# Eight experts of a mixture in one sequence: heavy blocks cut in halves between light ones

## The chip, the cores and the metric

The kernel runs on one core of a Trainium2 chip. The metric is the device time of one execution in microseconds (us). The engines are named as the profile names them: PE (TensorE, matmuls; PEld is its weight load), DVE (VectorE), ACT (ScalarE), POOL (GpSimd), SP (SyncE, which here only issues DMAs). "Part" means 1 MB of expert weights in this text, the unit in which they are loaded.

## What is computed

Two layers of a trunk with D = 1024 channels on T = 256 tokens. Each layer is a token mixer and a channel mixer; layer 0 has a dense channel mixer, layer 1 a mixture of 8 experts of which each token uses 2. All the change lies in that mixture. In the reference (cut):

```python
def _swiglu(t, w1, w3, w2):
    return (jax.nn.silu(t @ w1) * (t @ w3)) @ w2
...
    logits = (t @ w_router + b_router).astype(jnp.float32)
    top_val, top_idx = lax.top_k(logits, TOP_K)
    top_w = jax.nn.softmax(top_val, axis=-1)
    gates = jnp.sum(jax.nn.one_hot(top_idx, N_EXPERTS, dtype=jnp.float32) * top_w[..., None], axis=1)
    for e in range(N_EXPERTS):
        out = out + gates[:, e:e + 1].astype(t.dtype) * _swiglu(t, w1[e], w3[e], w2[e])
```

w1 and w3 of an expert are 1024 x 2816, w2 is 2816 x 1024, all in float32: 33 parts an expert, 264 in all. The kernel computes an expert only for the tokens that chose it.

## The kernel before

Up to the router the program is a fixed sequence. `route` (L1021) ranks the tokens of every expert and gives each expert a class `ov` by its count (up to 64, up to 128, up to 208, more). The loop at L1417 then goes over the experts in their own order. For each it loads the class into a register of all five engines and branches (L1426 to L1435) into one of four programs:

- `small` (L1168), up to 64 tokens. The tokens are gathered by a matmul with a one-hot matrix (`xg`, L1175) and turned (L1183). The 2816 hidden columns go in 11 blocks j. A block's first product `s` (L1200) takes two parts (w1 and w3 of 256 columns each), its second product `y` (L1218) one part of w2. The weights are the moving operand, straight from the loaded float32 part, and the 64 tokens are held in two column tiles of 64, which work on different columns. In order: transposes of the last block's gated values (`gT`, L1212; ACT copies them from PSUM, L1215), the first product of block j, the second product of block j - 1.
- `middle` (L1245), up to 128 tokens: the same with whole-array matmuls of 512 columns (`s` L1267, `gT` L1279, `y` L1286), and the weights split in a rounded high and a low half: ACT writes the high half `wh` (L210), DVE the low half `wl` (L211), in pieces of 128 x 1024.
- `many` (L1316), up to 208 or 256 tokens: tokens as the moving operand in the first product (`s` L1350 and L1352), weights moving in the second (`y` L1372), weights split as above, and gated values split by `split` (L248).
- After its last block an expert's rows are scaled (`ys`) and returned to the tokens by matmuls (`sc`, L1240, L1311, L1412), and `add_back` (L1140) adds them to `x_t`.

All weights come through SP's DMA queue into a ring of 15 slots of one part. `load_raw` (L186) takes the next slot in the order of use; `refill` (L178) is called after each stage and issues DMAs (L183) in that same order for the slots that are free. The first 15 parts are all of expert 0 and are issued before the router is done. `finish` (L1145) writes the output after the last expert.

## Time and profile before

| | us |
|---|---|
| median of 3 runs (1570.55 to 1571.85) | 1571.26 |
| the profiled execution | 1569.24 |
| its span in the trace | 1567.5 |
| PE busy in the span | 1371.7 (88%) |
| DVE busy | 881.6 (56%) |
| ACT busy | 605.2 (39%) |
| share of 16 DMA engines on SP's queue | 67.9% |

The span is the time between the first and the last record in the trace; the profiled execution's own time is 1.74 us longer. All rows read below are from this one execution. The experts occupy the span from 744 us to its end. PE's busy time comes from modelled ends of matmuls, so a busy PE is not necessarily at its full rate. The page counts bytes by queue (403.34 MB on SP's) and gives DMA's GB/s by slices, which is what the weight stream is read from.

### The profile page before, as it was taken

The numbers are of one execution on the slowest core, as the hardware profiler recorded it, in microseconds if no ns is written. First come the engines' busy times: TensorE is split into PE (matmuls) and PEld (weight loads), VectorE is DVE, ScalarE is ACT, GpSimd is POOL, SyncE is SP. The second block draws the span as 40 slices with busy tenths as digits, with TensorE's granted clock in tenths as the row PEclk, the third lists the DMA queues.
The fourth block names the chain that finished last, engine by engine and source line by source line (L and its number), as shares of the span: only waits on it lengthen the run. The fifth ranks groups of instructions, "written<-read, shape, count | busy, mean of one in ns | idle before, by whom it ended". The sixth has DMA issues, their size and how long they took to land.

```text
span 1567.5 us, 24755 instructions
## 1 busy us (share of the span) xinstructions
PE 1371.7 (88%) x9903; PEld 1139.8 (73%) x9903; DVE 881.6 (56%) x1443; ACT 605.2 (39%) x1115; POOL 318.9 (20%) x295
## 2 busy tenths in 40 slices
PE   4788999799998878988998949999799897979796
PEld 3676998699997777988665648988677574747474
DVE  7888679897777778687111036666588301010102
ACT  3453564354455534644111125555477211111112
POOL 0568019986201625050000000000000000000000
PEclk8898999799999899999998969999899998989899
DMA  7454356477776344479899975666399599999993
GB/s 285 174 190 160 125 188 212 136 258 240 261 257 223 133 136 135 166 244 403 359 419 416 419 290 189 215 203 203 130 348 351 212 420 416 419 416 419 417 419 122
DMA packets 60379, 420.37 MB, mean 268 GB/s; under 512 B 6688, under 2 KB 6688, under 8 KB 11296
## 3 DMA queue, kind: packets, MB, share of 16 engines
q1 hardware_dynamic: 56160, 403.34, 67.9%
q0 software_dynamic: 4032, 14.68, 2.8%
q8 instruction: 100, 1.64, 0.4%
q14 instruction: 87, 0.71, 0.1%
HBM read 416.94 MB, written 1.05 MB: 267 GB/s over the span
## 4 chain that ended last, share of the span: by engine, by line
PE 70%; DVE 18%; issue 6%; DMA 2%; ACT 2%; DVEq 0%; SPq 0%; ACTq 0%
PE s L1200 16%; PE mm L231 15%; PE y L1218 8%; DVE wl L211 6%; PE s L1350 4%; PE y L1372 4%; PE facc L971 3%; PE s L1267 3%; PE s L1352 2%; PE y L1286 2%; DMA raw<-in_w13m_dram 2%; DVE acc L309 1%; PE mm L716 1%; PE xg L1175 1%; DVE x_t L1141 1%
## 5 line engine op out<-in xcount | busy, mean ns | idle before, releaser
L211 DVE TENSOR_TENSOR wl<-raw,wh 128x1024 fp32r<-128x1024 f32 (+1 forms) x290 | 391.0, 1363 | 118.6 <-ACT wh L210 116.2
L210 ACT ACTIVATE wh<-raw 128x1024 fp32r<-128x1024 f32 (+1 forms) x290 | 302.3, 1057 | 252.1 <-PE mm L231 102.1
L231 PE MATMUL mm<-hh,wh 128*128 128x256 f32 x864 | 250.7, 292 | 5.1 <-ACT hh L250 2.9
L231 PE MATMUL mm<-hh,wl 128*128 128x256 f32 x864 | 249.7, 290 | 5.8 <-DVE wl L211 5.8
L1200 PE MATMUL s<-raw,xs 128*64 128x256 f32 x1920 | 250.1, 390 | 3.4 <-DVE xs L1187 3.4
L231 PE MATMUL mm<-hl,wh 128*128 128x256 f32 x864 | 249.5, 289 | 2.0 <-DVE hl L251 1.0
L1200 PEld LDWEIGHTS s<-raw,xs 128*64 128x64 f32 x1920 | 183.8, 140 | 48.2 <-issue 13.9
L1205 DVE TENSOR_TENSOR sg<-sg,s 64x256 f32<-64x256 f32 x66 | 28.0, 424 | 318.6 <-ACT sg L1204 269.8
L231 PEld LDWEIGHTS mm<-hh,wl 128*128 128x128 f32 x864 | 169.4, 196 | 9.8 <-DVE wl L211 6.3
L231 PEld LDWEIGHTS mm<-hh,wh 128*128 128x128 f32 x864 | 169.0, 196 | 9.4 <-ACT hh L250 3.3
L231 PEld LDWEIGHTS mm<-hl,wh 128*128 128x128 f32 x864 | 169.2, 196 | 3.7 <-DVE hl L409 1.5
L1218 PE MATMUL y<-raw,gT 128*64 128x512 f32 x520 | 143.1, 600 | 4.7 <-ACT gT L1215 4.7
L1204 ACT ACTIVATE sg<-s 64x256 f32<-64x256 f32 x66 | 24.8, 375 | 314.2 <-PE s L1200 314.2
L1350 PE MATMUL s<-xe,wh 128*128 128x416 f32 x352 | 107.2, 368 | 2.0 <-DVE sg L1360 1.7
L1352 PE MATMUL s<-xe,wl 128*128 128x208 f32 x352 | 91.0, 258 | 0.0
L309 DVE SCALAR_TENSOR_TENSOR acc<-raw,cond,acc 128x512 f32<-128x512 f32 x91 | 81.4, 894 | 1.6
L1218 PEld LDWEIGHTS y<-raw,gT 128*64 128x64 f32 x520 | 51.1, 136 | 40.9 <-issue 30.5
L317 POOL TENSOR_TENSOR araw<-araw,cond 128x1024 f32<-128x1024 f32 x28 | 62.3, 2229 | 71.8 <-DMA araw<-in_w_ada_dram 71.8
L1350 PEld LDWEIGHTS s<-xe,wh 128*128 128x128 f32 x352 | 66.2, 188 | 4.3 <-DVE sg L1360 2.4
L1352 PEld LDWEIGHTS s<-xe,wl 128*128 128x128 f32 x352 | 67.3, 191 | 0.4
L971 PE MATMUL facc<-fgh,wh 128*128 128x256 f32 x352 | 62.9, 281 | 0.2 <-ACT wh L210 0.2
L321 POOL TENSOR_TENSOR araw<-araw,araw 128x1024 f32<-128x1024 f32 x21 | 58.2, 2773 | 1.6
(513 smaller groups left out, 2369.0 us busy)
## 6 DMA issues: line engine op xcount, KB each, us to landing
raw<-in_w13m_dram SPq DMA_DIRECT2D x160, 1024.0 KB, 13.8
raw<-in_w2m_dram SPq DMA_DIRECT2D x87, 1024.0 KB, 13.7
raw<-in_w_ada_dram SPq DMA_DIRECT2D x32, 1024.0 KB, 5.1
raw<-in_w_in_dram SPq DMA_DIRECT2D x28, 1024.0 KB, 5.0
raw<-in_w13d_dram SPq DMA_DIRECT2D x22, 1024.0 KB, 5.0
late<-in_w13m_dram SPq DMA_DIRECT2D x16, 1024.0 KB, 16.2
araw<-in_w_ada_dram POOLq DMA_DIRECT2D x28, 512.0 KB, 4.6
raw<-in_w2d_dram SPq DMA_DIRECT2D x11, 1024.0 KB, 5.0
```

What stands on the lines that cost most here:

```text
L210: S.activation(hv, rv, AF.Copy)
L211: V.tensor_tensor(lv, rv, hv.bitcast(F32), op=ALU.subtract)
L231: PE.matmul(ps, lhsT=a[k][:, c0:c0 + P], rhs=b[:, k, :], start=k == 0 and i == 0 and o % 2 == 0, stop=k == n - 1 and i == 2 and o % 2 == 1)
L309: V.scalar_tensor_tensor(acc0, raw[:, k, :], c, acc0, op0=ALU.mult, op1=ALU.add)
L317: G.tensor_tensor(raw, raw, cond[:, r0:r0 + 2].unsqueeze(2).broadcast_to([P, 2, 512]), op=ALU.mult)
L321: G.tensor_tensor(acc, acc, raw, op=ALU.add)
L971: PE.matmul(o, lhsT=a[k][:, oc * P:(oc + 1) * P], rhs=b[:, k, :], start=j == 0 and oc % 2 == 0 and k == 0 and i == 0, stop=j == NB - 1 and ...
L1200: PE.matmul(ps[h][hf[h], 0:256], lhsT=xe4[:, k // 4, k % 4, :], rhs=w[k][:, 256 * h:256 * h + 256], start=k == 0, stop=k == KC - 1, tile_p ...
L1218: PE.matmul(y[h][hf[h], :], lhsT=g[:, k, :], rhs=w[k][:, 512 * h:512 * h + 512], start=j == 0 and k == 0, stop=j == NB - 1 and k == 1, til ...
L1350: PE.matmul(ps[:, 0:2 * nb], lhsT=hs[k][:, c], rhs=x.rearrange("p i s -> p (i s)"), start=k == 0, stop=False)
L1352: PE.matmul(ps[:, nb:2 * nb], lhsT=ls[k][:, c], rhs=x[:, 0, :], start=False, stop=k == KC - 1)
L1372: PE.matmul(y[b][n][0:s1 - s0, :], lhsT=g[:, k, s0:s1], rhs=w[w_][k][:, n * 512:n * 512 + 512], start=j == 0 and k == 0 and i == 0, stop=j ...
```

## The change

After the ranks, `ordered` (L1075 of the new kernel) sorts experts 1 to 7 by count and puts them in seven places behind expert 0 by `PLACE`. `si` holds which expert stands in each place; SP reads it into registers, and a part's DMA takes its expert from the register. `fi` says whether the counts fit the first list of `SIZES`, the second, or neither. A single branch (L1832) chooses: `straight` with the first list, with the second, or `general`, the old loop with its branches (now with a class of up to 32 besides).

`straight` is one sequence over all experts. Light experts (32 or 64 slots) follow each other in the order `LIGHT`, one block to a step, and the last block of one shares a step with the first of the next. A light expert of 32 uses four column tiles of 32, with 128 columns in a matmul of the first product and 256 in the second. Into these steps the 22 halves of each heavy expert are put (H1 its first product, H2 its second), a half every 1.1 steps: the 208-slot expert over steps 5 to 28, then three steps with none, the 128-slot expert over steps 32 to 55. All light blocks of steps 5 to 31 are of 32 slots; from step 33 on they are of 64. Gathers and returns are generators of which a piece runs after each step (`tick`). The ring has 14 slots, and only the 14 parts of expert 0 that fit are loaded before the sort. The sequence of parts in the ring follows the sequence of steps.

```diff
+SIZES = ((32, MANY, 32, 128, 64, 64, 64, 32), (64, MANY, 64, 128, 64, 64, 64, 64))
+HEAVY = (1, 3)
+LIGHT = (0, 2, 7, 5, 6, 4)
+LEAD, PACE, GAP = 5, 1.1, 3
...
+            w, e, (j, i), rows = parts[filled[0]]
+            if e and not experts:
+                return
+            src = w[0, j] if e == 0 else w[bass.ds(experts[e - 1], 1), j].squeeze(0)
+            if i is not None:
+                src = src[:, 4 * i:4 * i + 4, :]
             b = ring[filled[0] % len(ring)].rearrange("p (r c) -> p r c", r=rows)
             nc.sync.dma_start(b, src)
             filled[0] += 1
...
+        V.tensor_tensor(above[:, 0:7, 0:7], key[:, 1:8].unsqueeze(1).broadcast_to([P, 7, 7]),
+                        key[:, 1:8].unsqueeze(2).broadcast_to([P, 7, 7]), op=ALU.is_gt)
+        V.memset(rank[:, 0:1], -1.0)
+        V.reduce_sum(rank[:, 1:8], above[:, 0:7, 0:7], axis=AX.X)
...
+        def bring(o, row):
+            V.tensor_tensor(above, ow, row.unsqueeze(1).broadcast_to([P, 8, 8]), op=ALU.mult)
+            V.reduce_sum(o, above, axis=AX.X)
...
+        V.tensor_tensor(over, seq[:, 1:2, :].broadcast_to([P, 2, 8]), cov('limits').rearrange("p (a e) -> p a e", a=2),
+                        op=ALU.is_gt)
+        V.reduce_max(fl, over, axis=AX.X)
+        V.tensor_tensor(fi, fl[:, 0:1], fl[:, 1:2], op=ALU.add)
...
-        MR = 11
...
+        MR = 10
...
-        for e in range(NE):
-            rv = nc.values_load(ov[0:1, e:e + 1], engines=ENGS, min_val=0, max_val=3,
-                                skip_runtime_bounds_check_because="it is a sum of three comparisons")
...
-            with tc.If(rv < 1) as c:
-                arm(small)
-            with c.Else():
-                with tc.If(rv < 2) as c2:
-                    arm(middle)
-                with c2.Else():
-                    with tc.If(rv < 3) as c3:
-                        arm(lambda e: many(e, MANY))
-                    with c3.Else():
-                        arm(lambda e: many(e, T))
...
+        NARROW, WIDE = ("mm0", "mm0", "mm1"), ("mm0", "mm0", "mm1", "ms1", "ms1")
+        def wk(name):
+            return bank(work[0], name)
...
+            def turn_g():
+                ps = wk("gT")
+                for k in range(2 * n // 64):
+                    PE.transpose(ps[:, k * 64:(k + 1) * 64], st["sg"][hi, k * P:(k + 1) * P], ident[hi, hi],
+                                 tile_position=(64, 0))
+                st["g"] = mo.tile([P, 2, n], F32, name=nm("gS"), tag="gS", bufs=2)
+                S.activation(st["g"], ps[:, 0:2 * n].rearrange("p (k s) -> p k s", k=2), AF.Copy)
...
+            def stage1(j):
+                w = rows_of(w13m[0, j], KC, 512)
+                ps = wk("s1")
+                for k in range(KC):
+                    for g in range(G_):
+                        PE.matmul(ps[gr[g], 0:c_], lhsT=st["xe"][:, k // cb, k % cb, :], rhs=w[k][:, c_ * g:c_ * g + c_],
+                                  start=k == 0, stop=k == KC - 1, tile_position=(0, n * g))
                 refill()
...
+            def stage2(j):
+                if j == 0:
+                    st["y"] = bank(("mm1",), "y")
+                w = rows_of(w2m[0, j], 2, 1024)
+                for k in range(2):
+                    for h in range(G_):
+                        PE.matmul(st["y"][gr[h], 0:w_], lhsT=st["g"][:, k, :], rhs=w[k][:, w_ * h:w_ * h + w_],
+                                  start=j == 0 and k == 0, stop=j == NB - 1 and k == 1, tile_position=(0, n * h))
+                refill()
...
+            def stage1(j):
+                hs, ls = load_w(w13m[0, j], 8, 512, 2)
+                if n > P:
+                    gh, gl = (mo.tile([P, 2, n], F32R, name=nm("ghl"), tag="gT", bufs=2) for _ in range(2))
+                    for c in range(2):
+                        t = mo.tile([P, 2, n], F32, name=nm("sg"), tag="pt", bufs=2)
+                        for i in range(2):
+                            ps = wk("s1")
+                            o = slice((2 * i + c) * P, (2 * i + c + 1) * P)
+                            for k in range(KC):
+                                x = st["xe"][k // 4][:, k % 4]
+                                PE.matmul(ps[:, 0:2 * n], lhsT=hs[k][:, o], rhs=x.rearrange("p i s -> p (i s)"),
+                                          start=k == 0, stop=False)
+                                PE.matmul(ps[:, n:2 * n], lhsT=ls[k][:, o], rhs=x[:, 0, :], start=False, stop=k == KC - 1)
...
+                w = load_w(w2m[0, j], 2, 1024, 1)
+                if n > P:
...
+                for k in range(2):
+                    for b, (s0, s1) in enumerate(blk):
+                        for i, (g_, w_) in enumerate(((gh, 0), (gl, 0), (gh, 1))):
+                            for h in range(2):
+                                PE.matmul(st["y"][b][h][0:s1 - s0, :], lhsT=g_[:, k, s0:s1],
+                                          rhs=w[w_][k][:, h * 512:h * 512 + 512],
+                                          start=j == 0 and k == 0 and i == 0, stop=j == NB - 1 and k == 1 and i == 2)
+                refill()
...
+        def straight(sizes):
+            steps = []
+            for i, e in enumerate(LIGHT):
+                lo_ = 1 if i else 0
+                for j in range(lo_, NB):
+                    steps.append([("L", e, j)])
+                if i + 1 < len(LIGHT):
+                    steps.append([("L", LIGHT[i + 1], 0), ("L", e, NB)])
+                else:
+                    steps.append([("L", e, NB)])
+            at = LEAD
+            for e in HEAVY:
+                for t, j in [(t, j) for j in range(NB) for t in ("H1", "H2")]:
+                    steps[int(at)].append((t, e, j))
+                    at += PACE
+                at += GAP
+            order = []
+            for toks in steps:
+                for t, e, j in toks:
+                    if t == "L":
+                        order.extend(parts_of([(e, j)]))
+                    else:
+                        order.extend(p for p in parts_of([(e, j), (e, j + 1)])
+                                     if p[2][0] == j and (p[0] is w13m) == (t == "H1"))
+            parts[:] = order
...
+            for i, toks in enumerate(steps):
+                for t, e, j in toks:
+                    f = ex[e]
+                    if t == "L":
+                        if j == 0 and e:
+                            drain(gens[e])
+                        if j == 2 and ends:
+                            drain(ends.pop())
+                        f[1](j)
+                        if e == 0 and j == 1:
+                            gates_of(mo, gates, *picks)
+                            for tb in range(2):
+                                bring(gates[:, tb, :], gates[:, tb, :])
+                            work[0] = NARROW
+                            side.append(gens[HEAVY[0]])
+                        if j == 5 and e != LIGHT[-1]:
+                            side.append(gens[LIGHT[LIGHT.index(e) + 1]])
+                        if j == NB:
+                            ends.append(f[2]())
+                            side.insert(0, ends[0])
+                    elif t == "H1":
+                        drain(gens[e])
+                        f[1](j)
+                    else:
+                        f[2](j)
+                        if j == NB - 1:
+                            side.append(f[3]())
+                            if e != HEAVY[-1]:
+                                side.append(gens[HEAVY[HEAVY.index(e) + 1]])
+                            work[0] = NARROW
+                    if e == HEAVY[1] and t == "H1" and j == 0:
+                        work[0] = WIDE
+                tick()
+            drain()
...
+        fv = nc.values_load(fi[0:1, 0:1], engines=ENGS, min_val=0, max_val=2,
+                            skip_runtime_bounds_check_because="it is a sum of two comparisons")
+        start = turn[0], filled[0]
+        with tc.If(fv < 1, preferred_fallthrough_block=True) as c0:
+            straight(SIZES[0])
+        with c0.Else():
+            turn[0], filled[0] = start
+            with tc.If(fv < 2, preferred_fallthrough_block=True) as c1:
+                straight(SIZES[1])
+            with c1.Else():
+                turn[0], filled[0] = start
+                general()
```

On DVE, from the ranks to the branch. Before (`rov` is the class, `rrk` the ranks, `pm` the one-hot matrix of expert 0):

```order
L1050 SCALAR_TENSOR_TENSOR rlg_7885<-rank_7902,rlg_7885 128x8
L1051 SCALAR_TENSOR_TENSOR rov_7908<-rank_7902,rlg_7885 128x8
L1054 TENSOR_TENSOR rrk_7912<-rank_7902,roh_7898 128x16
L1055 TENSOR_SCALAR rrk_7912<-rrk_7912 128x16
L1119 TENSOR_SCALAR pm_7920<-co_t,rrk_7912 128x128 x2
L1418 TENSOR_LOAD rov_7908
L1426 COMPARE_AND_BRANCH
```

After, the last of the added operations (`rseq` takes the ranks in the new order, `rfi` is the flag):

```order
L1093 TENSOR_TENSOR rabove_7925<-row_7927,rov_7906 128x64
L1094 TENSOR_REDUCE rseq_7928<-rabove_7925 128x8
L1098 CAST rsi_7937<-rseq_7928 128x16
L1101 TENSOR_TENSOR rover_7939<-rseq_7928,co_t 128x16
L1093 TENSOR_TENSOR rabove_7925<-row_7927,rrk_7911 128x64
L1103 TENSOR_REDUCE rfl_7940<-rover_7939 128x2
L1094 TENSOR_REDUCE rseq_7928<-rabove_7925 128x8
L1104 TENSOR_TENSOR rfi_7941<-rfl_7940 128x1
L1093 TENSOR_TENSOR rabove_7925<-row_7927,rrk_7911 128x64
L1094 TENSOR_REDUCE rseq_7928<-rabove_7925 128x8
L1829 TENSOR_LOAD rfi_7941
L1832 COMPARE_AND_BRANCH
```

The sort stands whole between the ranks and the branch, which the old order reaches two operations after the ranks.

On PE, where a block of the 208-slot expert passes from its first product to its second. Before:

```order
L1350 MATMUL s_1439_9638<-xe_9317,wh_9631 128x416
L1352 MATMUL s_1439_9638<-xe_9317,wl_9632 128x208
L1372 MATMUL y_9370<-wh_9725,ghl_9566 128x512
L1372 MATMUL y_9371<-wh_9725,ghl_9566 128x512
L1372 MATMUL y_9370<-wh_9725,ghl_9567 128x512
```

After (`gT`, `y` with 256 columns and `s` with 128 are the light expert's, `sc` the return of a finished light expert):

```order
L1642 MATMUL s_1261_9236<-xe_8127,wh_9167 128x416
L1644 MATMUL s_1261_9236<-xe_8127,wl_9168 128x208
L1589 MATMUL sc_9263<-geS_8209,ys_9261 128x256
L1589 MATMUL sc_9266<-geS_8209,ys_9261 128x256
L1531 MATMUL gT_9275<-co_t,sgS_9139 128x64
L1680 MATMUL y_8585<-wh_9327,ghl_9171 128x512
L1680 MATMUL y_8586<-wh_9327,ghl_9171 128x512
L1556 MATMUL y_9317<-raw_7656,gS_9277 32x256
L1589 MATMUL sc_9269<-geS_8209,ys_9261 128x256
L1589 MATMUL sc_9272<-geS_8209,ys_9261 128x256
L1556 MATMUL y_9317<-raw_7656,gS_9277 32x256 x4
L1541 MATMUL s_1269_9279<-raw_7654,xeS_8527 32x128 x16
```

Between the two heavy products there now stand matmuls of two light experts, in another shape of tile.

On ACT at the same place. Before (`sg` are copies of the first product from PSUM, `ghl` the split of the gated values, `wh` a piece of weights):

```order
L1361 ACTIVATE sg_10124<-sg_10124 128x208
L1359 ACTIVATE sg_10124<-s_1498_10054 128x208
L1361 ACTIVATE sg_10133<-sg_10133 128x208
L210 ACTIVATE wh_10179<-raw_7652 128x1024
L1359 ACTIVATE sg_10133<-s_1499_10055 128x208
L210 ACTIVATE wh_10183<-raw_7653 128x1024
L250 ACTIVATE ghl_10122<-sg_10124 128x208
```

After (`gS` is the copy of the light block's transposes, `sgS` its gated values):

```order
L1645 ACTIVATE sg_9216<-s_1260_9217 128x208
L222 ACTIVATE wh_9327<-raw_7657 128x1024
L1647 ACTIVATE sg_9216<-sg_9216 128x208
L222 ACTIVATE wh_9331<-raw_7657 128x1024
L222 ACTIVATE wh_9444<-raw_7661 128x1024
L222 ACTIVATE wh_9448<-raw_7661 128x1024
L1645 ACTIVATE sg_9216<-s_1261_9236 128x208
L1534 ACTIVATE gS_9277<-gT_9275 128x64
L262 ACTIVATE ghl_9171<-sg_9216 128x208
```

The light block's copy now stands in ACT's queue behind pieces of heavy weights and the last PSUM copy of the heavy half.

## Rows read from the trace of the kernel before

**Rows 1.** Stretches: length; busy PE, PEld, DVE, ACT, POOL; PEclk, DMA share, GB/s.

```profile
822.30:908.00 85.70, 72.85 (x506) 48.03 (x506) 10.11 (x25) 9.52 (x26) 0.00 (x0) 0.90 1.01 417
908.00:924.00 16.00, 0.00 (x0) 0.00 (x0) 2.18 (x6) 2.95 (x3) 0.00 (x0) 0.50 0.95 370
924.00:1112.00 188.00, 183.45 (x1080) 164.66 (x1080) 117.91 (x175) 97.33 (x163) 0.00 (x0) 0.99 0.56 189
1112.00:1230.00 118.00, 106.88 (x474) 83.98 (x474) 93.26 (x105) 76.28 (x92) 0.00 (x0) 0.96 0.79 295
...
1318.50:1400.40 81.90, 72.74 (x506) 47.93 (x506) 10.13 (x26) 9.52 (x26) 0.00 (x0) 0.94 1.01 418
```

**Rows 2.** Chain of waits, light experts: start us, us, engine and line.

```profile
1318.53 8.38 PE s L1200 x64
...
1336.61 2.81 PE s L1200 x25
1339.41 0.27 PE gT L1212 x2
1339.68 0.79 PE s L1200 x5
1340.47 1.80 PE y L1218 x8
1342.28 2.81 PE s L1200 x25
...
1400.42 8.39 PE s L1200 x64
```

**Rows 3.** Chain of waits: second products of the two crowded experts' blocks.

```profile
955.86 5.53 PE y L1372 x24
971.01 5.58 PE y L1372 x24
...
1157.59 2.32 PE y L1286 x10
...
1166.51 2.32 PE y L1286 x10
```

**Rows 4.** Timeline, end of routing: start us, us, engine, line, operation, out<-in.

```profile
743.43 0.17 DVE L1054 TENSOR_TENSOR rrk<-rank,roh 128x16 f32<-128x16 f32 x1
743.63 0.17 DVE L1055 TENSOR_SCALAR rrk<-rrk 128x16 f32<-128x16 f32 x1
...
751.18 6.15 PE L1200 MATMUL s<-raw,xs 128*64 128x256 f32 x40 [0.52 <-DVE xs L1187]
...
754.81 0.33 SPq L183 DMA_DIRECT2D raw<-in_w13m_dram  x1
```

**Rows 5.** The end of the span: chain of waits, then timeline.

```profile
1546.38 1.99 PE y L1218 x8
...
1560.66 2.58 SPq L1166 DMA_DIRECT2D out_dram<-wh  x4
```

**Rows 6.** Timeline, conditioning stage: matmuls in four column tiles of 32.

```profile
26.50 0.59 PEld L282 LDWEIGHTS adar<-raw,condr 128*32 128x32 f32 x16
26.51 1.07 PE L282 MATMUL adar<-raw,condr 128*32 128x256 f32 x16
```

**Rows 7.** Groups by shape, 924 to 1112 us: weight splits (busy, mean ns | idle).

```profile
L211 DVE TENSOR_TENSOR wl<-raw,wh 128x1024 fp32r<-128x1024 f32 x61 | 74.7, 1224 | 42.3 <-ACT wh L210 42.3
...
L210 ACT ACTIVATE wh<-raw 128x1024 fp32r<-128x1024 f32 x61 | 64.3, 1056 | 43.0 <-PE s L1352 15.0 <-issue 10.9 <-DVE wl L211 9.0
```

**Rows 8.** Chain of waits: the gather of the 208-slot expert.

```profile
924.14 7.68 PE xg L1333 x48
```

**Rows 9.** Chain of waits between experts, where no engine is waited for.

```profile
904.31 4.71 issue
...
909.68 7.95 issue
...
1389.13 5.06 issue
```

More of the change, by code (lines that the diff above doesn't have):

```diff
@@ L173, in wtile @@
             i -= b
-    ring, parts, turn, filled = [], [], [0], [0]
+    ring, parts, experts, turn, filled = [], [], [], [0], [0]
     def refill():
         while filled[0] < min(len(parts), turn[0] + len(ring)):
-            src, rows = parts[filled[0]]
+            w, e, (j, i), rows = parts[filled[0]]
[4 more added lines that the diff above has]
+                src = src[:, 4 * i:4 * i + 4, :]
             b = ring[filled[0] % len(ring)].rearrange("p (r c) -> p r c", r=rows)
@@ L1076, in gates_of, with parts_of @@
         V.tensor_tensor(gates, o0, o1, op=ALU.add)
+    def parts_of(steps):
+        r = []
+        for e, j in steps:
+            if j < NB:
+                r.extend((w13m, e, (j, i), 4) for i in range(2))
+            if j:
+                r.append((w2m, e, (j - 1, None), 2))
+        return r
     def moe_begin():
@@ L1136, in back_of @@
             return ge, gs
-        slots_of(0)
+        slots_of(0, rk0)
+        bring, si, fi, rk = ordered(mo, key, ov, rk0)
+        for e in range(1, NE):
+            experts.append(nc.values_load(si[0:1, 0, e:e + 1], engines=[mybir.EngineType.SP], min_val=0, max_val=NE - 1,
+                                          skip_runtime_bounds_check_because="it is a sum over a one-hot row"))
         def add_back(e, ch, y):
@@ L1188, in small @@
-            y = [ms_ps("y", 0) for _ in range(2)]
+            xe4, ps4 = (t[:, 0:KC * n].rearrange("p (c g s) -> p g c s", c=cb, g=G_) for t in (xe, ps))
+            for g in range(G_):
+                V.tensor_tensor(xe4[:, g], ps4[:, g], sh[:, cb * g:cb * g + cb].unsqueeze(2).broadcast_to([P, cb, n]),
+                                op=ALU.add)
+            y = ms_ps("y", 0)
             def rows_of(src, rows, cols):
-                n = min(rows, 2048 // cols)
-                return [w[:, r, :] for i in range(0, rows, n)
-                        for w in (load_raw(src[:, i:i + n, :], n, cols),) for r in range(n)]
+                m = min(rows, 2048 // cols)
+                return [w[:, r, :] for i in range(0, rows, m)
+                        for w in (load_raw(src[:, i:i + m, :], m, cols),) for r in range(m)]
@@ new lines, in general, with arm @@
+        def general():
+            parts[:] = parts_of([(e, j) for e in range(NE) for j in range(NB + 1)])
+            for e in range(NE):
+                rv = nc.values_load(si[0:1, 1, e:e + 1], engines=ENGS, min_val=0, max_val=4,
+                                    skip_runtime_bounds_check_because="it is a sum of four comparisons")
+                def arm(f):
+                    turn[0], filled[0] = first
+                    f(e)
+                    refill()
+                first = turn[0], filled[0]
+                with tc.If(rv < 2, preferred_fallthrough_block=False) as c:
+                    with tc.If(rv < 1, preferred_fallthrough_block=False) as c1:
+                        arm(lambda e: small(e, 32))
+                    with c1.Else():
+                        arm(lambda e: small(e, 64))
+                with c.Else():
+                    with tc.If(rv < 3, preferred_fallthrough_block=False) as c2:
+                        arm(middle)
+                    with c2.Else():
+                        with tc.If(rv < 4) as c3:
+                            arm(lambda e: many(e, MANY))
+                        with c3.Else():
+                            arm(lambda e: many(e, T))
```

337 lines of the change are left out of this document (268 added, 69 removed).

## The prediction

> **What bounds the kernel now.** I read the busy times by stretch first [rows 1]. The change touches only what follows the router, the span from about 743 us on. There the column for bytes per second splits the experts in two kinds. While an expert with up to 64 tokens runs, the weights arrive at 417 to 418 GB/s and the DMA share is 1.01: that stretch is as long as its transfers. While the two crowded experts run, at 924 to 1112 us and 1112 to 1230 us, the rate falls to 189 and 295 GB/s, and TensorE is busy 183.45 of 188.00 us and 106.88 of 118.00 us: these are as long as their matmuls. So one resource waits for the other in every stretch, and never the same one. The chain of waits gives the sizes. Two light experts start at 1318.53 and 1400.42 us, 81.9 us for 33 parts of 1 MB, 2.48 us a part. Inside, the blocks that find their weights landed take 1342.28 - 1336.61 = 5.67 us [rows 2], where three parts need 7.45: a light expert wants 62 us of TensorE and 82 us of DMA. A block of the 208-slot expert takes 971.01 - 955.86 = 15.15 us and one of the 128-slot expert 1166.51 - 1157.59 = 8.92 us [rows 3]; times eleven that is 167 and 98 us of TensorE for the same 82 us of DMA.
>
> **The first landing and the tail.** The ring's first refill after the prefetch is issued at 754.81 us, and the first light matmuls run from 751.18 us [rows 4]. At the other end the last block's second product starts at 1546.38 us and the output's DMA starts at 1560.66 us, with the span ending at 1567.5 [rows 5]; the last product takes 1.99 us, so 19.1 us lie between its end and the span's end. The order puts an expert of the 32 class last; its return to the tokens is as small a job, so I leave this tail as it is.
>
> **Which path is taken.** The list is decided by the token counts. Working the reference's router out for its inputs gives 20, 54, 194, 113, 23, 40, 43, 25 for the eight experts. Sorted, expert 0 apart, they are 194, 113, 54, 43, 40, 25, 23, and these fit the first list: 32, 208, 32, 128, 64, 64, 64, 32. The trace agrees as far as it can show: one expert ran as 208, one as 128, six as 64.
>
> **The change, part by part.**
>
> *Sort and flag.* About 17 more small VectorE operations stand in a chain ahead of the branch. Two of today's, one waiting for the other, start 0.20 us apart [rows 4]. Seventeen in line are 3.4 us, up to 6 if those on 64 numbers take longer. I take 4.3: the first expert starts its matmuls at 751.18 + 4.3 = 755.5, and the first refill leaves at about 758.5 (a little less later, since the 32-wide first block frees its parts sooner). Only 14 parts can be loaded ahead, since the later ones need the sort: one fewer than before, 2.5 us of DMA.
>
> *DMA's floor.* 264 parts less 14 leave 250, at 2.48 us each 620 us: the last lands at 1379 us, its product ends 2 us later, and with the tail the span is 1400. Nothing in the trace shows the queue at its full rate beside the two crowded experts, so this is a lower bound. A part's source now comes from a register, one more SP instruction for each; today's issue takes 0.33 us [rows 4] of the 2.48 that a part has. The trace has no DMA of this kind; up to 2.1 us more for each would stay hidden, and I take nothing.
>
> *Light experts of 64.* Three remain, 33 blocks of 5.67: 187 us of TensorE.
>
> *Light experts of 32.* Three, 33 blocks, now in four column tiles instead of two. The trace has four such tiles in the conditioning stage: 16 records of 128x256 in 1.07 us, and their 16 weight loads in 0.59, 0.037 us each [rows 6]. A light block's first product is 64 such records, half as wide, so it can't be faster than about 64 x 0.037 = 2.4 us; its second product is 16 records of 256, 0.95 us; the transpose stays at 0.27 [rows 2]. That makes 3.6 us a block, 119 in all. Ends: half of today's streaming, 1.8 + 0.9 + 0.27 = 3.0, and no gain at all, 5.67. I take 3.6, since the four tiles' rows are the same kind of instruction.
>
> *Heavy halves.* The same matmuls, 11 x 15.15 = 167 us. The 128-wide blocks lose what they wait for weights now: 8.6 of 8.92 remain, 95 us. A weight piece costs ScalarE 1.06 us and VectorE 1.22 after it [rows 7]; a heavy block has six pieces, 7.4 us of VectorE in the 18.8 us that a 208-wide block shares with a light one, and in the 14 us beside a 64-wide one. Neither engine becomes the bound on average; singly they can be late.
>
> *Side work.* The gathers, gate columns and returns are the same kinds as before, on TensorE's path: for the 208 class 7.68 us for the first 48 gathers of 64 [rows 8], so about 10, and 6 for its return; 9 for the 128 class; 6 for a 64, 3 for a 32. Together 50 us.
>
> *What goes.* Seven of the eight branch points, at which TensorE sits idle: 5.06 us before a light expert, 4.71 and 7.95 on the way into the 208-wide one [rows 9]. Where weights are the bound those 5 us were covered, so they give nothing; the sums above simply don't contain them.
>
> *What is added: waits between two chains.* TensorE takes a light block's transpose, first product and second product in turn, with a heavy half after each step or so. A light second product must wait for ScalarE's copy of the transposed gates, and in the new order that copy stands behind a heavy part's weight pieces and PSUM copies. Queued behind TensorE's wait are the light block's remaining matmuls and the heavy half after them. One weight piece is 1.06 us of ScalarE [rows 7], so a block can lose 0 to 1 us. I take 0.45 for each of 22 heavy blocks, 10 us; 8 us for weight splits not ready in the 128-wide stretch, 3 us of low clock at the start, 6 us for the tile shapes (next paragraph): 27 us, bounds 5 and 95 (the last is a rival, below).
>
> *Tile shapes.* TensorE changes between whole-array and 64- or 32-column matmuls some 270 times instead of some 160. The pair of transposes inside a light block is such a change and back, and takes 0.27 us with its work [rows 2]; 0.13 us for each change is then the most, 15 us for the 110 added, and nothing the least. I take 6, nearer to what one change alone can be with the transposes' own work in the row. The Trainium skill says of this, in TensorEngine Tiling (Array Packing), Tiling Modes, that a change of tiling mode drains TensorE, which speaks against this interleaving; by the upper price the sum would be 9 us higher, and the light block's rows show no more than that.
>
> **The sum.** TensorE from 755.5: 187 + 119 + 167 + 95 + 50 + 27 = 645, so the last product ends at about 1400 and the span at 1419.6. The DMA's floor is 1400, 20 us less, and by this sum TensorE never runs out of weights: after the 208-wide expert it is some ten parts ahead, inside the ring's 14. So TensorE is the bound by a small margin. The profiled execution of before lies 1.74 us over its span and the median of the runs 3.76 us over it (1571.26 against 1567.5): the forecast is 1419.6 + 3.8 = **1423 us**.
>
> **The rivals.**
>
> *Waits between the chains.* The two engines that split weights also serve the light chain. If each of the 44 heavy halves loses 1.5 us more (one weight piece on each engine in front of what TensorE wants [rows 7]) that is 66 us: up to 1489. For it: VectorE stood idle 42 us for ScalarE in the 208-wide expert [rows 7]. Against: TensorE was busy 183.45 of 188 us all the same [rows 1]. Chance 0.15.
>
> *Four tiles bring nothing.* If a 32-wide block takes 5.67 us like a 64-wide one, 33 x 2.07 = 68 us are added, 1491. Against it stand [rows 6]. Chance 0.04.
>
> *TensorE falls to its lower clock while it waits for weights.* In the last ten blocks and wherever DMA is late, TensorE works in bursts. Now, in light experts, it has 62 us of such work in 82 and its granted clock is 0.90 to 0.94, and it stood at 0.50, the 1.2 GHz level, only at 908 to 924 us, with nothing to do for 16 us [rows 1]. At the lower level a 64-wide block would take about 11.3 us for 7.45 us of weights; in the last stretch of eleven blocks that is 42 us, 1465. Chance 0.03. The Trainium skill has this rule in TensorE: Matmul & The Clock Gate, HAM oscillation: waits for DMA between short bursts throw the clock back, each time. The trace of before doesn't bear it out at these lengths of wait.
>
> *The lists aren't met.* Then the old branches run, with the sort on top and a ring one slot shorter: 1572 to 1580. The counts speak against it. Chance 0.02.
>
> *The other side: 32-wide tiles run one after another.* A 32-wide block streams as many columns as a 64-wide one. If its four tiles don't overlap at all, where two do now, both products take twice today's time: 7.2 + 3.6 + 0.27 = 11.1 us. Then 33 blocks cost 247 us more than forecast, and the result is 1670, slower than before. It decides from about 8.1 us a block on ((1571 - 1423) / 33 = 4.5 over 3.6). Against: [rows 6] show four tiles' records overlapping. Chance 0.03.
>
> **How the numbers follow.** My forecast, 1423, has its own band from 1400 (TensorE's waits small and the DMA's floor reached, or a little better) to 1445, with a chance of 0.73. The range 1400 to 1465 adds half of the first rival, 0.80 together. Faster by over 0.2% (about 3 us, what a measurement of this kernel can tell from no change): 0.73 + 0.15 + 0.04 + 0.03 = 0.95. Within 0.2%: 0.01 of the fallback. Slower: 0.04.
>
> **What the profile after would show.** Right: a stretch from about 760 to 1400 us in which DMA holds 390 GB/s or more and TensorE is busy over nine tenths, with no fall at 920 us; light blocks of 32 about 3.6 us apart where no heavy half lies between; heavy blocks 18 to 20 us apart with their light step; the two sides finishing together. Wrong: TensorE idle in pieces of about 1 us released by ScalarE's gate copy or by a weight split, 44 times over; a granted clock of half in the last ten light blocks; DMA at less than 390 GB/s while its queue has free slots, which would mean that its floor is higher than the light experts show.

## The result, and the profile after

The changed kernel takes 1451.54 us in the median of four runs (1444.21 to 1454.24), the kernel before 1571.55 beside it: a ratio of 0.9227 (95% interval 0.9192 to 0.9262). The forecast was 1423 us, the range 1400 to 1465. So the direction and most of the size came as reckoned, and 28 us of the expected 148 did not come. The profiled execution took 1451.57 us, its span is 1449.8, against the 1419.6 of the sum: 30.2 us to be explained.

Where the span goes now is seen in the stretches of the expert part. The columns are those of [rows 1]; the five rows are the first light blocks, the 208-slot expert among blocks of 32, the gap, the 128-slot expert among blocks of 64, and the last ten light blocks.

```profile
761.65:790.20 28.55, 28.55 (x579) 24.18 (x578) 11.68 (x21) 9.34 (x20) 0.00 (x0) 0.94 0.89 355
790.20:1054.00 263.80, 252.03 (x2937) 206.81 (x2934) 122.59 (x206) 104.26 (x203) 0.00 (x0) 0.99 1.01 415
1054.00:1082.00 28.00, 27.76 (x431) 22.54 (x430) 15.16 (x31) 9.78 (x20) 0.00 (x0) 1.00 1.01 420
1082.00:1355.90 273.90, 255.32 (x1495) 152.78 (x1494) 104.96 (x141) 87.39 (x140) 0.00 (x0) 0.98 1.01 415
1355.90:1430.10 74.20, 65.67 (x477) 35.08 (x476) 11.23 (x26) 8.46 (x24) 0.00 (x0) 1.00 0.63 243
```

Two things are to be seen. The rows at 189 and 295 GB/s [rows 1] are gone: the weights arrive at 415 GB/s while both crowded experts compute. And TensorE is busy in every stretch, but not without holes: 11.8 us are missing in the second, 18.6 in the fourth, 8.5 in the last, where DMA is already running out of work. The chain of waits over two of the last light blocks shows one kind of hole (start us, us, engine and line):

```profile
1405.46 0.39 ACT sgS L1546
1405.87 0.43 DVE sgS L1547
...
1406.35 0.33 PE gT L1531 x2
1406.68 1.87 PE y L1556 x8
1408.55 3.48 PE s L1541 x32
1412.05 0.39 ACT sgS L1546
1412.46 0.43 DVE sgS L1547
...
1412.94 0.34 PE gT L1531 x2
```

Against [rows 2] the order has turned. Before, the transposes `gT` stood in the middle of the next first product, so the gating `sgS` of ScalarE and VectorE was long done. Now they stand straight behind the first product whose gating they need: TensorE sits for 0.9 us in each such block, which takes 6.6 us instead of 5.67. The table of waits names it (engine and line, what it waited for: us in total, times, longest):

```profile
PE gT L1531 <- DVE sgS L1547: 18.0, 21, 1.0
PE y L1556 <- ACT gS L1534: 7.6, 10, 1.6
...
PE y L1680 <- ACT wh L222: 1.6, 2, 1.3
PE s L1655 <- ACT wh L222: 1.4, 1, 1.4
```

The second row is the wait that the prediction had in mind. The chain of waits shows it at the end of a 208-wide first half, after light matmuls of 32 slots:

```profile
810.32 0.20 PE gT L1531
810.52 1.88 PE s L1541 x64
812.41 0.86 PE y L1556 x16
...
822.17 0.35 ACT sg L1647
822.53 0.96 ACT wh L222
...
824.50 1.04 ACT wh L222
825.54 0.23 ACT sg L1645
825.77 0.12 ACT gS L1534
...
825.93 1.07 PE y L1556 x16
```

ScalarE has pieces of heavy weights and PSUM copies ahead of `gS`, the copy that the light second product waits for. The first three rows also give the price of a block of 32 slots: 0.20 + 1.88 + 0.86 = 2.9 us, not 3.6.

TensorE's clock fell too. By the trace's clock records it stood at 0.5, the 1.2 GHz level, for 17.0 us between the first and the last expert matmul, 10.2 of them in the 128-wide stretch. Two places there:

```profile
1232.50:1236.20 3.70, 3.70 (x11) 2.81 (x9) 3.13 (x4) 0.91 (x1) 0.00 (x0) 0.54 1.02 425
1349.00:1355.60 6.60, 6.60 (x15) 4.14 (x14) 2.44 (x4) 0.00 (x0) 0.00 (x0) 0.51 0.96 398
```

In the first, heavy matmuls of 512 columns start every 0.43 us; elsewhere in the stretch the median is 0.23. So a stretch at 0.5 does about half the work of one at full clock: an estimate, which is used below.

Ahead of the experts the sort did what was forecast. In the timelines, the kernel before in the first row and the changed kernel in the others:

```profile
742.64 0.20 PE L1043 MATMUL rank<-roh,tri_b 128*128 128x8 bf16 x2 [3.73 <-DVE roh L1038]
...
748.97 0.20 PE L1055 MATMUL rank<-roh,tri_b 128*128 128x8 bf16 x2 [3.74 <-DVE roh L1050]
...
761.65 3.56 PE L1541 MATMUL s<-raw,xeS 128*32 128x128 f32 x64
...
763.65 1.96 SPq L195 DMA_DIRECT2D raw<-in_w13m_dram  x2
```

From the ranks to the first expert matmul are 12.7 us; before, they were 8.5 ([rows 4] have the other end, 751.18). That is 4.1 us more for 4.3 forecast. But the ranks themselves come 6.3 us later than before.

### The profile page after: what moved, and what is told of

Same layout as the page of the kernel before. It is cut to its first block, busy times and chain, and to the rows that moved or that the text cites. A ratio compares the mean times of both kernels' runs of the same rounds, so it can differ in the third digit from the quotient of the medians.

```text
span 1449.8 us, 27552 instructions
## 1 busy us (share of the span) xinstructions
PE 1287.1 (89%) x11256; PEld 1054.8 (73%) x11256; DVE 882.0 (61%) x1477; ACT 591.9 (41%) x1111; POOL 316.8 (22%) x295
## 4 chain that ended last, share of the span: by engine, by line
PE 71%; DVE 17%; ACT 5%; issue 4%; DMA 2%; DVEq 0%; ACTq 0%
PE mm L243 17%; PE s L1541 12%; PE y L1680 6%; PE y L1556 5%; PE s L1642 5%; DVE wl L223 5%; PE s L1655 4%; PE facc L983 4%; ACT wh L222 2%; PE s L1644 2%; DVE acc L321 1%; PE sc L1589 1%; PE yps L888 1%; PE gT L1531 1%; PE mm L728 1%
## 5 line engine op out<-in xcount | busy, mean ns | idle before, releaser
L223 DVE TENSOR_TENSOR wl<-raw,wh 128x1024 fp32r<-128x1024 f32 (+1 forms) x290 | 383.8, 1346 | 132.4 <-ACT wh L222 116.7
L222 ACT ACTIVATE wh<-raw 128x1024 fp32r<-128x1024 f32 (+1 forms) x290 | 298.4, 1055 | 214.9 <-PE mm L243 103.1
L1541 PE MATMUL s<-raw,xeS 128*32 128x128 f32 (+1 forms) x2944 | 176.6, 315 | 0.9 <-PE y L1556 0.6
L1541 PEld LDWEIGHTS s<-raw,xeS 128*32 128x32 f32 (+1 forms) x2944 | 122.1, 121 | 47.3 <-issue 7.2
L1547 DVE TENSOR_TENSOR sgS<-sgS,s 64x128 f32<-64x128 f32 (+1 forms) x66 | 23.6, 358 | 160.1 <-ACT sgS L1546 159.7
L1642 PE MATMUL s<-xe,wh 128*128 128x416 f32 x352 | 107.7, 370 | 0.0
L1546 ACT ACTIVATE sgS<-s 64x128 f32<-64x128 f32 (+1 forms) x66 | 21.3, 323 | 201.5 <-PE s L1541 191.5
L1556 PE MATMUL y<-raw,gS 128*32 128x256 f32 (+1 forms) x744 | 95.6, 455 | 7.9 <-ACT gS L1534 7.6
L1680 PE MATMUL y<-wh,ghl 128*128 128x512 f32 (+1 forms) x264 | 76.9, 411 | 1.6 <-ACT wh L222 1.6
L1680 PEld LDWEIGHTS y<-wh,ghl 128*128 128x128 f32 (+1 forms) x264 | 45.1, 179 | 26.3 <-issue 6.9
```

The costliest lines, as they stand in the source:

```text
L222: S.activation(hv, rv, AF.Copy)
L223: V.tensor_tensor(lv, rv, hv.bitcast(F32), op=ALU.subtract)
L1541: PE.matmul(ps[gr[g], 0:c_], lhsT=st["xe"][:, k // cb, k % cb, :], rhs=w[k][:, c_ * g:c_ * g + c_], start=k == 0, stop=k == KC - 1, tile_p ...
L1556: PE.matmul(st["y"][gr[h], 0:w_], lhsT=st["g"][:, k, :], rhs=w[k][:, w_ * h:w_ * h + w_], start=j == 0 and k == 0, stop=j == NB - 1 and k ...
L1642: PE.matmul(ps[:, 0:2 * n], lhsT=hs[k][:, o], rhs=x.rearrange("p i s -> p (i s)"), start=k == 0, stop=False)
L1680: PE.matmul(st["y"][b][h][0:s1 - s0, :], lhsT=g_[:, k, s0:s1], rhs=w[w_][k][:, h * 512:h * 512 + 512], start=j == 0 and k == 0 and i == 0, ...
```

## The experiments

Each kernel is the changed one with one edit. Because the stages ahead of the router vary, as the first and the last run show, I compare the length from the first expert matmul to the end of the span: 688.1 us in the changed kernel, of which 273.4 lie between the first and the last matmul of the 128-slot expert and 74.0 behind it, up to the last light second product.

**The changed kernel again.**

> The changed kernel once more, beside the kernel before on one chip, as the measure for the other runs of this call and for one question: its first matmuls after the router came 6.3 us later than forecast, and the stages ahead of the router, whose order on TensorE is unchanged, had drifted by that much already. Theory A, the drift belongs to that one execution or chip: the class of the tokens is then ranked at about 743 us, as before, and the time is about 1445. Theory B, the change causes it (other places in memory, another ring): it comes again, ranks at about 749 us and a time of about 1451.

It took 1445.67 us (1440.38 to 1447.67), the kernel before on the same chip 1574.34 (1564.7 to 1582.34, seven runs). The ranks came at 747.35 us, and the expert part was 685.2 us long, with 270.3 and 74.0. Neither theory's number, 743 or 749, is the ranks' time; it lies between. So the expert part repeats within 3 us, and the stages before it are taken up again in the last run.

The 3 us go with the clock, which stood at 0.5 for 9.2 us in this profile and 17.0 in the first. Counted in the trace from the start of each matmul to the start of the next, idle time left out, TensorE works 625.3 us here and 628.7 in the first profile. With the time at 0.5 taken as half, this is 620.6 and 620.2.

**The transposes behind the second product.**

> Only the order on TensorE differs: the transposes of a light block's gated values are queued behind the second product of the block before, instead of straight behind the first product whose gating they need. Theory 1, in the changed kernel TensorE is the bound and loses 18.0 us (21 waits of up to 1.0 us) at these transposes: some 18 us less, about 1433. Theory 2, the weights' stream sets the end (its last part landed at 1406.5 us, and 250 parts of 2.49 us need 622): the wait only changes its place and the time stays within 5 us of the changed kernel's.

```diff
-                for k in range(2 * n // 64):
...
+                with tc.issue_after(last_y[0]) if last_y else nullcontext():
+                    for k in range(2 * n // 64):
...
+                last_y[:] = [i_.ins]
```

Here `i_` is the last matmul of the light `stage2`, and what the block traces on TensorE is queued behind it.

It took 1454.63 us (1451.59 to 1459.81; the unchanged program beside it 1445.67, with ranks 9.4 us earlier in its profile), and the expert part 688.6: nothing gained, as theory 2 has it, but not for its reason. Fourth and last stretch of this kernel:

```profile
1089.40:1372.80 283.40, 258.74 (x1494) 153.93 (x1493) 104.76 (x141) 86.96 (x140) 0.00 (x0) 0.98 0.99 399
1372.80:1438.00 65.20, 64.77 (x477) 35.05 (x476) 11.22 (x26) 8.45 (x24) 0.00 (x0) 1.00 0.73 289
```

The last blocks lose their holes: 65.2 us for 74.2, TensorE busy throughout. The 128-wide stretch gives it all back, 283.4 us for 273.9, and the stream is slower in it, so it isn't the stream that sets the pace. In the timeline of that stretch:

```profile
1158.00 0.34 PE L1534 MATMUL gT<-co_t,sgS 64*128 64x64 f32 x2
...
1158.43 0.28 ACT L1537 ACTIVATE gS<-gT 128x128 f32<-128x128 f32 x1 [1.66 <-PE gT L1534]
...
1158.60 3.89 ACT L222 ACTIVATE wh<-raw 128x1024 fp32r<-128x1024 f32 x4
...
1159.70 0.73 PE L1659 MATMUL s<-wh,xe 128*128 128x512 f32 x2 [1.37 <-ACT wh L222]
```

The later transpose makes `gS` late; `gS` stands at the head of ScalarE's queue and keeps it idle for 1.66 us; the heavy weight pieces behind it come late, and TensorE waits 1.37 us for them at the crowded expert's first matmul. The table of waits has the 18.0 us of `gT` gone, and these rows, which stood at 1.6 us or less, have grown:

```profile
PE s L1659 <- ACT wh L222: 8.2, 6, 1.4
PE y L1684 <- ACT wh L222: 7.1, 6, 1.4
...
PE s L1659 <- DVE wl L223: 3.4, 8, 0.5
```

By the rows of the two stretches, TensorE's idle time accounts for 6.1 of the 9.5 us that the 128-wide one grew by. The other 3.4 are longer matmuls; 13.7 us at the lower clock, against 10.2, make about half of these.

**The same in the last ten steps alone.**

> The transposes are queued behind the second product only in the last nine light blocks, where no crowded expert's half stands between. In the run that did it everywhere these last blocks took 65.2 us instead of 74.2, and the 128-wide stretch 283.4 instead of 273.9. Theory 1, ScalarE's queue couples the two chains, so the order pays where there is no heavy half and costs where there is one: about 9 us less from the first expert matmul to the end (688 and 685 us in the changed kernel's two traces), with the 128-wide stretch as in the changed kernel. Theory 2, TensorE's total is fixed by something else, such as the stream: the gain is given back elsewhere, as before, and the length stays at 685 to 688.

```diff
+                with tc.issue_after(last_y[0]) if now[0] > 56 else nullcontext():
```

The edit takes in the transposes of steps 57 to 66, ten of them; at nine of these TensorE waited in the changed kernel.

1437.09 us (1432.57 to 1446.12), the expert part 679.8: 8.3 us shorter than in the changed kernel's first profile and 5.4 shorter than in its second, with 273.3 us in the 128-wide stretch as in the first and 65.4 behind it. Time at the lower clock is 16.8 us, as in the first profile, so the 8.3 are the ones to compare, and theory 1 foretold them within a microsecond: the order pays where no heavy half stands between.

**The copy on VectorE, with and without that order.**

> The transposes are queued behind the second product in every light block, and the copy of the transposed gates is made by VectorE instead of ScalarE. Theory 1, the 9.5 us lost in the 128-wide stretch came from that copy, which waited for TensorE at the head of ScalarE's queue with heavy weight pieces behind it: these waits (8.2 and 7.1 us at the heavy products' first matmuls) go, the 128-wide stretch returns to 265 to 274 us, the last blocks stay at 65, and the whole is 10 to 18 us shorter than the changed kernel. Theory 2, VectorE's queue holds the low halves of the same pieces, so the wait only moves there: the stretch stays near 283 us.

```diff
-                S.activation(st["g"], ps[:, 0:2 * n].rearrange("p (k s) -> p k s", k=2), AF.Copy)
+                V.tensor_copy(st["g"], ps[:, 0:2 * n].rearrange("p (k s) -> p k s", k=2))
```

With both, 1429.96 us (1426.5 to 1431.06), a ratio of 0.9089 to the kernel before (0.9041 to 0.9136), where the changed kernel has 0.9227 and 0.9178. The expert part is 672.1 us, 13 to 16 shorter than the changed kernel's, and theory 1 holds:

```profile
1078.20:1343.10 264.90, 251.65 (x1492) 149.91 (x1490) 110.32 (x165) 81.82 (x116) 0.00 (x0) 1.00 1.01 421
1343.10:1408.50 65.40, 65.02 (x478) 35.11 (x476) 14.05 (x36) 5.79 (x14) 0.00 (x0) 1.00 0.75 307
```

Of the 16 us against the first profile, 12.8 are idle time of TensorE (26.3 us for 39.1); most of the rest goes with the clock, at 0.5 for 10.8 us instead of 17.0.

> Only the copy of the transposed gates moves from ScalarE to VectorE; the order on TensorE is left to the same rules as in the changed kernel. Theory 1, two separate costs: the transposes' wait behind their own first product (18.0 us) stays, and only the waits that came from ScalarE's queue go (7.6 us at the light second products, some 4 us at heavy weight pieces): 675 to 682 us from the first expert matmul to the end, against 688.1 and 685.2. Theory 2, the copy's engine was all that mattered: about 672 us, as in the run that made both edits.

With the copy on VectorE alone, in the order of the changed kernel, the expert part is 683.9 us (one run; 1448.79 us with ranks at 750.4): the 128-wide part falls to 266.0, the last blocks stay at 73.9, and 18.6 us of waiting at the transposes remain. That is 2 us above what theory 1 gave and 12 above theory 2. So there are two costs, nearer to theory 1, and the order pays among the heavy halves only once ScalarE's queue is free of the copy: alone, the edits bring nothing and 1 to 4 us, together 13 to 16.

**Half of the light first product.**

> The light experts' first product leaves out every second of its eight channel blocks; all weights are still loaded, in the same order. It takes about 33 x 1.75 + 33 x 0.95 = 89 us of matmuls off TensorE. Theory 1, TensorE is the bound and the stream's own floor lies at 764 + 622 + 2 + 20 = 1408 us: the span falls to 1408 to 1415, and no further. Theory 2, the stream can't hold its rate beside the crowded experts: the span stays above 1425 with DMA as the bound. Theory 3, waits between the two chains set the end: it stays above 1430 with TensorE idle and the ring full.

```diff
-                for k in range(KC):
+                for k in range(0, KC, 2):
...
```

1414.42 us, a span of 1412.7, an expert part of 654.5. All of it up to 1380 us runs at the stream's rate:

```profile
800.00:1380.00 580.00, 519.96 (x3765) 343.82 (x3763) 244.31 (x385) 201.45 (x369) 0.00 (x0) 0.97 1.01 421
```

This is theory 1 by its number and its mechanism: the stream keeps its full rate beside the crowded experts, and the changed kernel stays above its floor because of TensorE. But the floor is higher than reckoned. The expectation counted from a first refill at 764 us, and here it left at 759.4; the last part landed at about 1390 us, 632 behind the first expert matmul, where the prediction's sum has 1379 and 755.5, that is 623.5.

**The crowded experts in one piece.**

> The interleaving undone and all else kept (one branch, 32-wide tiles, sort, ring): the 22 halves of each crowded expert run in one piece, at light steps 5 and 32. Theory 1, what the change gains is mainly that weights of light experts are loaded while crowded ones compute: about 100 us of that stream is then lost again (167 and 100 us of TensorE for 82 us of weights each, less what the ring holds), 1520 to 1540 us. Theory 2, the gain is mainly from the branches and the narrower tiles: within 30 us of the changed kernel.

```diff
-LEAD, PACE, GAP = 5, 1.1, 3
+LEAD, PACE, GAP = 5, 0.0, 27
```

1540.97 us; the expert part is 787.6 us long, 99.5 more. The 208-slot expert and the light blocks behind it:

```profile
779.80:972.20 192.40, 170.52 (x947) 144.80 (x944) 101.42 (x147) 89.28 (x149) 0.00 (x0) 0.99 0.58 216
972.20:1158.60 186.40, 142.87 (x2424) 97.95 (x2422) 32.73 (x91) 23.20 (x75) 0.00 (x0) 0.81 0.97 401
```

The old picture is back [rows 1]: 216 GB/s with a busy TensorE, then 401 GB/s with a TensorE that waits. This is theory 1, a microsecond above its range: some 100 of the 120 us gained are the interleaving's.

**All light experts with 64 slots.**

> The first list takes 64 slots for every light expert, so that no block runs in four column tiles; all else is kept. Theory 1, a 32-wide block takes 3.0 us in the trace and a 64-wide one 5.7: 33 x 2.7 = 89 us more of TensorE, of which nothing is hidden, since TensorE is the bound from the first block: about 1530 to 1545. Theory 2, the weights' stream is the bound in the 208-wide stretch (DMA share 1.01 there), and narrower tiles only lengthen the waits for it: less than 40 us more.

```diff
-SIZES = ((32, MANY, 32, 128, 64, 64, 64, 32), (64, MANY, 64, 128, 64, 64, 64, 64))
+SIZES = ((64, MANY, 64, 128, 64, 64, 64, 64), (64, MANY, 64, 128, 64, 64, 64, 64))
```

1514.61 us, an expert part of 758.5, 70.4 more. 62 of them lie between the 208-slot expert's first matmul and the 128-slot expert's:

```profile
797.90:1151.90 354.00, 349.21 (x2277) 249.91 (x2275) 142.09 (x233) 118.78 (x223) 0.00 (x0) 1.00 0.88 341
```

Neither theory has the number: the extra matmuls show up by 2.1 us a block and not 2.7, but far more than the 40 that a bound stream would leave, and the stream is below its rate here. TensorE is the bound.

**Halves in pairs.**

> A crowded block's second half and the next block's first half now follow each other, every 2.2 light steps, instead of one half every 1.1: the same work with half as many changes between the two kinds of matmul (some 44 fewer). Theory 1, a change of tile shape costs TensorE 0.15 to 0.2 us (a light first product of 32 matmuls takes 3.63 us behind a heavy half and 3.48 behind a light one): 6 to 8 us less in the two heavy stretches together (263.8 + 273.9 us). Theory 2, the rows of the light blocks show all there is and the change itself is free: within 3 us. Theory 3, what matters is the room between the halves of a block for ScalarE and VectorE: longer, with more waits for weight pieces.

```diff
                     steps[int(at)].append((t, e, j))
-                    at += PACE
+                    if t == "H1":
+                        at += 2 * PACE
```

1451.9 us, an expert part of 693.4, 5 to 8 longer, though the last blocks took 65.5 us (the crowded expert ends a step later here, and one block fewer is left behind it). Adding up as above, TensorE works 630.2 us in this kernel and 628.7 in the changed one; idle are 42.5 and 39.1. The clock stood at 0.5 for 22.7 us here, against 17.0; with this time taken as half, the work is 618.8 us, against 620.2 and 620.6. And between the first and the last light matmul the trace has 232 changes of tile shape instead of 259, 27 fewer and not 44. So they save 1 to 2 us of TensorE's work, not the 6 to 8 of theory 1, and the lower clock and the waits take more than that. Of theory 3 only the longer time is seen, since waits for weight pieces aren't among the rows that grew: the transposes' wait went from 18.0 us to

```profile
PE gT L1531 <- DVE sgS L1547: 25.5, 27, 1.4
```

because more light blocks now follow each other directly.

**The kernel before once more.**

> The kernel before, profiled once more, for the stages ahead of the router, which the change leaves alone. Theory A, their length differs from one execution to the next: the tokens' ranks come at another time than the 742.6 us of the first profile, anywhere in the 739 to 757 us that the other eight profiles show, while the stretch from the first expert matmul to the end stays within 3 us of the 816.3 of the first profile. Theory B, the change lengthens them: 742 to 744 us again.

1571.99 us. In its timeline:

```profile
745.17 0.20 PE L1043 MATMUL rank<-roh,tri_b 128*128 128x8 bf16 x2 [3.73 <-DVE roh L1038]
...
753.70 6.65 PE L1200 MATMUL s<-raw,xs 128*64 128x256 f32 x44 [0.52 <-DVE xs L1187]
```

The ranks come 2.5 us later than in its first profile, while from the first expert matmul to the span's end (1570.2) it is 816.5 us, against 816.3. The same program's early stages thus differ by execution. The ten profiles with the change's early stages have the ranks from 739 to 757 us, and the kernel before lies inside that. Whether the change adds a microsecond or two there on average is left open.

## Why the prediction was right, and where it was off

**The bound and the direction** were right. The stream runs while the crowded experts compute, and TensorE is the bound by a small margin: with less work for it the expert part falls from 688.1 to 654.5 us, and up to 1380 us it then runs at the stream's rate. The stream's own floor was some 8 us too low in the sum, as that run shows. Most of the gain is what the prediction said it is, undone by running the heavy blocks in one piece.

**The time** lies in the range, but above the band of 1400 to 1445 that the prediction gave to its own sum.

**The 30.2 us of the span**, step by step: 6.3 came ahead of the ranks, which the sum took as unchanged, and which differ that much from execution to execution. The sort cost 4.1 for 4.3. From the first expert matmul at 761.65 to the end of the last product at 1430.1 are 668.5 us, for 645 forecast: 23.5. Behind it lie 19.7 for 19.1.

**The 645** were 618 us of matmuls in five terms, 6 for changes of shape, 3 for the low clock and 18 for waits. Added up from start to start as above, the light products and transposes took 293 us where 187 + 119 = 306 were forecast: 104 for the 32-wide blocks, which were nearer to my lower end, and 189 for the 64-wide. The heavy products took 279 for 262, the side work 56 for 50. So the matmuls took 629 us, with the changes of shape and the low clock in them, where 627 were forecast; that these errors nearly cancel is luck. With the time at 0.5 taken as half they took 620, and the low clock some 8.5 instead of 3. TensorE's idle time was 39 for the 18 of waits, and this is most of the 23.5 us.

**The step that failed** is the one on waits between two chains, for which the sum has 18 us and the runs show 39. It had the right engine and the right queue, ScalarE's copy behind heavy weight pieces, at about the right size (7.6 us for 10). It missed that the new order puts a light block's transposes straight behind its own first product, 18.0 us in 21 places: in the order by rows `gT` does stand in front of the second product `y`, and I read from it who is queued, not how far the gating was from its use. And these waits aren't a sum of separate terms: taking one away made others grow, through ScalarE's queue, until the copy left that queue too.

**The 32-wide blocks** are the term that was mis-sized the other way. The prediction took 64 weight loads of 0.037 us, 2.4 us, as the least for the first product; it took 1.88 us, and the second 0.86 for 0.95.

**The heavy products' 17 us** stay partly open. The 208-wide blocks took 171.7 us for 167, the 128-wide 107.7 for 95. In the 128-wide stretch 10.2 us at the lower clock are worth about 5 by the estimate above, not all of them in heavy matmuls. Changes of shape are a part too: the first whole-array matmul behind a light second product starts 0.52 us after the light one before it (the median of nine places in the trace), where a light first product in the same tiles starts 0.42 us after it (eleven places), and a light first product starts 0.33 us behind a whole-array matmul, where another whole-array one starts 0.23 us behind it. That is some 0.1 us a change, within the prediction's 0 to 0.13. The Trainium skill has a reason for such a pause (TensorEngine Tiling (Array Packing), Tiling Modes: a change of mode drains TensorE). No run here shows that this is the cause, and 27 fewer changes saved 1 to 2 us in all.

**Two readings** were wrong without moving the sum. A half every 1.1 steps puts 2.2 light blocks beside a heavy block, not one; the heavy blocks start some 25 us apart (790.2 to 1039.0 and 1082.1 to 1333.9 us, ten distances each), not 18 to 20. And the kernel before had its clock at 0.50 at other places than 908 to 924 us, such as the start of a light expert:

```profile
822.80:836.40 13.60, 7.55 (x26) 3.21 (x28) 1.94 (x5) 0.59 (x1) 0.00 (x0) 0.50 1.02 413
```

**The rivals.** The first, waits between the chains at 1.5 us more for each heavy half, didn't come as it was meant: TensorE waited 7.6 us for ScalarE's gate copy and 4.5 for weight pieces in all, where the sum already had 10 and 8. The waits that came are at the transposes, nine of the 21 in the last light blocks, behind all heavy halves. The low clock didn't come there, with a granted clock of 1.00, but it did for 17.0 us elsewhere. Four tiles do bring something, 70 us. The list fitted, and the light tiles overlap.

## What to carry to other kernels

Where one stretch is bound by its transfers and another by its matmuls, laying them side by side can be worth most of the difference, here some 100 us. The longer of the two sums is then the floor, and the waits between the chains come on top. Look in the new order for how many instructions lie between an operand's making on another engine and its use, in each kind of step. And where two chains share an in-order queue, a wait taken from one engine can come back through that queue on the other chain: edit the queue and the order together. Before a small difference between two runs is put down to an edit, count the time that TensorE spent at the lower clock in each.

## What the runs showed of the hardware

A light block with four column tiles of 32 takes 2.9 us where two of 64 take 5.67, with the same number of streamed columns: 64 records of 128 columns in 1.88 us, below the 2.4 us that I had worked out from weight loads.

With the crowded experts in one piece, the light blocks behind them waited for weights in bursts and the granted clock was 0.81 on average, while it is 0.98 to 1.00 in the interleaved sequence from 790 us on. Those blocks ran at the stream's rate, 401 GB/s; what the clock cost there isn't shown by itself.

In the seven profiles with the same matmuls and the heavy halves among light blocks, TensorE's work from start to start is 625.0 to 631.4 us. With the time at 0.5 of the clock taken as half it is 617.6 to 621.5: the difference between these runs is their idle time and their clock.

The weights' stream held 421 GB/s for 580 us while ScalarE and VectorE split weights and TensorE computed, as much as it had beside light experts alone [rows 1].
